# Branch A's queries as a third Strassen chunk, gates multiplied outside the streamed matmuls, and low weight halves made by accumulating DMAs

## The chip, the cores and the metric

One program runs on one core of a Trainium2 chip. The metric is the device time of an execution in microseconds, from its first to its last instruction with what lies around them; lower is better. A kernel's time is the median of three runs.

## The reference, cut to what matters

One layer of a decoder trunk: 512 tokens of width 2048, everything in fp32. One wide projection feeds three attention branches (A sparse, B latent, C over 256 memory tokens), each branch output is multiplied with SiLU of its own gate path z, projected to 2048, weighted with a sigmoid merge gate, summed, and projected out with a residual.

```python
h = rms_norm(x, norm_g[l])
proj = h @ w_in[l]                                   # 512x2048 @ 2048x13712
(aq, ak, av, az, iq, ik, iw, bcq, bckv, bkpe, bz, cq, cz, gates) = jnp.split(proj, IN_OFFSETS, axis=-1)
aq = rms_norm(aq.reshape(bsz, seq, A_HEADS, A_HEAD_DIM), a_q_norm_g[l])
o_a = dsa_attention(aq, ak, av, iq, ik, iw, positions, rel_bias).reshape(bsz, seq, A_WIDTH)
qb = (rms_norm(bcq, b_q_lat_norm_g[l]) @ w_b_uq[l]).reshape(bsz, seq, B_HEADS, B_QK_DIM)
kv = (rms_norm(bckv, b_kv_lat_norm_g[l]) @ w_b_ukv[l]).reshape(bsz, seq, B_HEADS, B_NOPE + B_V)
...
o_b = mla_attention(qb, kb, vb).reshape(bsz, seq, B_WIDTH)
mkv = rms_norm(mem, mem_norm_g[l]) @ w_mem_kv[l]
o_c = memory_attention(cq, ck, cv).reshape(bsz, seq, C_WIDTH)
u = jnp.stack([o_a * jax.nn.silu(az), o_b * jax.nn.silu(bz), o_c * jax.nn.silu(cz)], axis=2)
y_br = jnp.einsum('bsnw,nwd->bsnd', u, w_branch[l])
g = jax.nn.sigmoid(gates.reshape(bsz, seq, N_BRANCH, d))
merged = jnp.einsum('bsnd,bsnd->bsd', g, y_br)
x = x + merged @ w_out[l]
```

## The kernel before, in words

**Numbers in halves.** Every streamed product is made of three matmuls in a faster 32-bit format: each operand x is split into a high half (a copy into that format) and a low half (x minus the high half), and high·high, high·low and low·high are added up in PSUM. Activations are split once. Weights are split as they stream in: SP loads a tile of two 128-row blocks by 512 columns (`wraw`, 512 KB), ACT copies it to `whi`, DVE subtracts to get `wlo` (`split`).

**The stream.** `stream()` walks a list of chunks. A chunk is one block of 512 output columns; a job is one weight tile of it. A plain job is 24 matmuls of 128x512 (2 row blocks, 4 PSUM banks of ring `pg`, 3 products). A Strassen chunk takes two column blocks at once and forms 7 products where 8 would be needed, on sums of weight quarters that DVE makes from the raw tiles; its jobs are 12 matmuls. `LOOK` says how many jobs ahead of the matmuls the halves are prepared: 2 for a plain job, 3 for a Strassen job; `whi` and `wlo` have 3 buffers each, with one more (`extra`) for every fourth Strassen job.

**The order of chunks.** Memory keys and values; the first half of the indexer's queries; `bckv`; the Strassen chunks (cq0, cq1) and (bcq, akv) from `rows_chunk`; six Strassen chunks for the merge gates; the indexer's second half; uq and ukv (B's up-projections); **aq0 and aq1** (A's queries, plain, 16 row blocks each); the z chunks C0, C1, A0, A1, B0, B1; twelve branch chunks (four each for C, B, A, 8 row blocks each); two Strassen out chunks. The attention of C, B and the indexer runs between the matmuls of the stream up to the end of the z chunks, A's heads in the branch chunks of C and B.

**What sets the order.** `run` takes one step of the stream at a time and, after each, lets the attention threads go on as far as a planner's clock finds their data ready. The order of every engine and of every DMA queue is fixed by that when the program is built; each engine, and each queue, then works strictly in that order. SP carries the weight loads; the Pool queue carries spills to DRAM, reloads and attention loads.

**The end of a chunk.** `evac` empties the four banks of `pg`; the next chunk begins in the same four banks, in turn, right behind. In a z chunk each bank takes a tanh on ACT and a multiply-add on DVE, (tanh(z/2)+1)·z, which is twice SiLU. `silu_to_dram` (A's z before) stores that in DRAM as `sp_s`. `gated_chunk` (C's and B's z before) goes on: the attention output o comes back from DRAM (`zo`), `gated` multiplies, `halves` splits, and the two halves of u are stored as `sp_u`. `u_thread` later loads u for C (on SP) and B (on Pool); for A it loads s and o into `u_s` and `u_o`, multiplies and splits there.

**Between B and A.** When B's last head is done, A's preparation is issued on the Pool queue: positions (`pi`, `ki`), bias tables (`rb`), keys and values (`akv`), then the first A queries (`a_q`). The tile of `pi` takes memory that the B heads used, so its DMA waits for the last store of B's output (`sp_oB`).

**Names in the rows.** All instructions are recorded through one helper, so all have line 140; they are told apart by tiles. `hh`, `hl` are the halves of h, `hS` Strassen sums of it; `pg`, `pn` PSUM rings of the stream; `pa`, `pb`, `ra` those of attention; `mE`, `mO`, `mA` the halves for the out chunks; `wT` weight sums for these, made in DRAM and in part by accumulating DMAs on the Pool queue.

## Time and profile before

| | |
|---|---|
| time, median of three runs | 1877.44 us (1874.31, 1877.44, 1878.06) |
| profiled execution, own time | 1878.15 us |
| its span | 1876.3 us |
| PE busy | 1852.0 us (99%), 9341 matmuls |
| DVE, ACT, POOL busy | 1375.1 (73%), 860.7 (46%), 219.9 us (12%) |
| mean granted TensorE clock | 0.998 |
| DMA | 372.95 MB; the hardware queue of SP 37.0%, the software queue of Pool 25.1% of 16 engines' span |

PE is the engine that sets the time: what it does not spend in matmuls is 24.3 us of 1876.3. An engine's busy time elsewhere matters only where PE stands waiting for it. In rows of a timeline the bracket at the end tells how long the engine was idle before that instruction and what ended the wait; matmuls are pipelined, so that the distance between two starts, not the duration, is what one takes.

### The profile page before, as it was taken

How to read it: one execution, taken by the hardware profiler on the slowest of the kernel's cores; microseconds unless marked ns; L12 is line 12 of the kernel's file. 1: busy time of each engine (PE TensorE's matmuls, PEld its weight loads, DVE VectorE, ACT ScalarE, POOL GpSimd, SP SyncE). 2: the span in 40 equal slices, each digit the busy share in tenths (PEclk: the TensorE clock that was granted, in tenths of full speed). 3: DMA queues.
4: the chain of work that ended last, by engine and by line, in shares of the span. 5: the costliest groups of instructions: out<-in, count | busy, mean ns of one | idle time of the engine just before them, and what ended most of it. 6: DMA issues, size and time to landing. Idle time of an engine off the chain costs nothing. (4 is left out here: it accounts for less than half of the span.)

```text
span 1876.3 us, 25087 instructions
## 1 busy us (share of the span) xinstructions
PE 1852.0 (99%) x9341; PEld 1546.2 (82%) x9341; DVE 1375.1 (73%) x2156; ACT 860.7 (46%) x1429; POOL 219.9 (12%) x332
## 2 busy tenths in 40 slices
PE   8999999999999999999999999999999999999999
PEld 6789888888888888879888888878888888887787
DVE  5577877778777786765567789994788886667655
ACT  6543554454444444436846654433332324244442
POOL 1000010100001101021211111002012121210000
PEclk9999999999999999999999999999999999999999
DMA  7754558867667697575734435435565665946783
GB/s 263 248 183 143 163 188 317 205 210 213 188 194 290 225 254 202 173 240 164 262 111 142 129 113 180 149 109 166 171 239 191 200 215 175 316 158 211 259 270 123
DMA packets 155049, 372.95 MB, mean 199 GB/s; under 512 B 14560, under 2 KB 19568, under 8 KB 153648
## 3 DMA queue, kind: packets, MB, share of 16 engines
q1 hardware_dynamic: 111696, 220.36, 37.0%
q0 software_dynamic: 43200, 150.99, 25.1%
q8 instruction: 73, 1.20, 0.3%
q14 instruction: 48, 0.39, 0.1%
q10 hardware_dynamic: 32, 0.01, 0.0%
HBM read 308.63 MB, written 96.24 MB: 216 GB/s over the span
## 5 line engine op out<-in xcount | busy, mean ns | idle before, releaser
L140 DVE TENSOR_TENSOR wlo<-wraw,whi 128x1024 fp32r<-128x1024 f32 (+2 forms) x285 | 344.2, 1210 | 214.6 <-ACT whi L140 212.6
L140 ACT ACTIVATE whi<-wraw 128x1024 fp32r<-128x1024 f32 (+2 forms) x285 | 297.6, 1047 | 383.6 <-PE pg L140 160.2
L140 PE MATMUL pg<-whi,u 128*128 128x512 f32 x640 | 218.3, 400 | 0.0
L140 PE MATMUL pg<-hh,whi 128*128 128x512 f32 x512 | 207.0, 404 | 2.5 <-DVE stage L140 1.7
L140 PE MATMUL pg<-hh,wlo 128*128 128x512 f32 x512 | 200.7, 392 | 0.0
L140 PE MATMUL pg<-hl,whi 128*128 128x512 f32 x512 | 200.0, 391 | 0.0
L140 PE MATMUL pg<-whi,hh 128*128 128x512 f32 x384 | 151.8, 395 | 0.0
L140 PE MATMUL pg<-whi,hl 128*128 128x512 f32 x384 | 149.8, 390 | 0.0
L140 PE MATMUL pg<-wlo,hh 128*128 128x512 f32 x384 | 149.6, 390 | 0.0
L140 PEld LDWEIGHTS pg<-whi,u 128*128 128x128 f32 x640 | 120.3, 188 | 23.2 <-DVE yg L140 0.3
L140 ACT ACTIVATE whi<-sraw 128x1024 fp32r<-128x1024 f32 x79 | 83.2, 1058 | 98.5 <-DVE sraw L140 45.4
L140 DVE TENSOR_TENSOR wlo<-sraw,whi 128x1024 fp32r<-128x1024 f32 x79 | 96.4, 1224 | 42.5 <-ACT whi L140 42.1
L140 PE MATMUL pn<-whi,hS 128*128 128x512 f32 x384 | 126.0, 389 | 0.0
L140 PE MATMUL pg<-whi,hS 128*128 128x512 f32 x384 | 126.0, 389 | 0.0
L140 PE MATMUL pg<-wlo,u 128*128 128x512 f32 x320 | 125.1, 391 | 0.8 <-DVE wlo L140 0.8
L140 PE MATMUL pn<-whi,hl 128*128 128x512 f32 (+1 forms) x320 | 121.4, 379 | 0.0
L140 PE MATMUL pn<-wlo,hh 128*128 128x512 f32 (+1 forms) x320 | 121.4, 379 | 0.0
L140 PE MATMUL pn<-whi,hh 128*128 128x512 f32 (+1 forms) x320 | 121.4, 379 | 0.0
L140 PEld LDWEIGHTS pg<-hh,whi 128*128 128x128 f32 x512 | 96.8, 189 | 21.9 <-DVE stage L140 2.6
L140 PEld LDWEIGHTS pg<-hh,wlo 128*128 128x128 f32 x512 | 96.4, 188 | 21.1
L140 PEld LDWEIGHTS pg<-hl,whi 128*128 128x128 f32 x512 | 96.8, 189 | 17.3
L140 DVE TENSOR_TENSOR wlo<-T,whi 128x1024 fp32r<-128x1024 f32 x64 | 78.2, 1222 | 33.9 <-ACT whi L140 33.7
(450 smaller groups left out, 3956.9 us busy)
## 6 DMA issues: line engine op xcount, KB each, us to landing
wraw<-w_in SPq DMA_DIRECT2D x161, 512.0 KB, 3.9
sraw<-w_in SPq DMA_DIRECT2D x79, 512.0 KB, 4.5
wT<-w_out POOLq DMA_DIRECT2D x24, 1024.0 KB, 20.5
wraw<-w_branch SPq DMA_DIRECT2D x48, 512.0 KB, 4.4
wraw<-w_mem_kv SPq DMA_DIRECT2D x32, 512.0 KB, 5.3
yg<-sp_g POOLq DMA_DIRECT2D x24, 512.0 KB, 6.1
so<-wT SPq DMA_DIRECT2D x20, 512.0 KB, 5.7
wT<-wT POOLq DMA_DIRECT2D x8, 1024.0 KB, 13.8
```

Source lines behind the costliest of these rows:

```text
L140: return f(*a, **k)
```

## The change

Five things are done at once.

1. aq0 and aq1 leave the plain list and become a third `rows_chunk`, behind (bcq, akv) and ahead of the merge gates. `C0` gets the start condition that aq0 had.
2. `gated_chunk` is gone. All six z chunks (C, A, B as before) end in `silu_to_dram`. `u_thread` loads s and o, on SP, into the four `stage` buffers, and `gate` multiplies and splits them, for all three branches, shortly ahead of the branch chunk that reads u.
3. For the six z chunks (48 jobs) and the branch chunks of C and B (32 jobs), marked `dma`, the low halves come from `halves_by_dma`: ACT copies raw to `whi`, ACT writes −`whi` into `wlo`, and a DMA on the Pool queue that accumulates adds the raw weights, read from DRAM a second time, to `wlo`. `add_upto` issues it two jobs ahead of the job's matmuls. The DVE subtraction of these 80 jobs is gone.
4. `LOOK` is 3 for all jobs; `whi` and `wlo` have 4 buffers everywhere; `so` has 2 instead of 4; the flag `m sums` is gone.
5. The outputs of the attention heads are stored by ACT's DMA queue instead of Pool's, and the tile `o` is that of the probabilities.

The whole program has 9293 matmuls in place of 9341 (all of the 48 are 128x512 ones of the stream), 192 `wlo` subtractions on DVE in place of 269, and 80 more copies to `wlo` on ACT. On the Pool queue 80 accumulating DMAs of 512 KB come in, and 8 stores of `sp_s`; 16 stores of `sp_u`, 4 loads of u, 8 of `zo`, 8 of `u_s` and `u_o` and 40 stores of o go. On SP's queue 24 loads of s and o come in and 4 of u go; ACT's queue gets the 40 stores.

```diff
 class Kern:
-    LOOK = 2
+    LOOK = 3
...
+        def new_pair():
+            return [self.wp.tile([P, 2, 512], F32R, name=n, tag=n, bufs=4) for n in ("whi", "wlo")]
+
+        def halves_by_dma(jb, src):
+            h, l = new_pair()
+            nc.scalar.activation(h, src, AF.Copy)
+            nc.scalar.activation(l, h, AF.Copy, scale=-1.0)
+            jb["hl"] = (h, l)
+            (w,), row = jb["raws"][0]
+            st["adds"].append((st["nprep"], lambda: nc.gpsimd.dma_start(
+                l, w[row:row + 2 * P, :].rearrange("(k p) c -> p k c", p=P), accum_op=OP.add)))
+
+        def add_upto(n):
+            while st["adds"] and st["adds"][0][0] <= n:
+                st["adds"].pop(0)[1]()
+
         def halves(jb, src, w):
-            if jb.get("extra") and jb["ready"]:
-                h, l = [self.bp.tile([P, 2, 512], F32R, name=n, tag="yg", bufs=2) for n in ("whi", "wlo")]
-            else:
-                pool, bufs = (self.gp, 1) if jb.get("extra") else (self.wp, 3)
-                h = pool.tile([P, 2, 512], F32R, name="whi", tag="whi", bufs=bufs)
-                l = pool.tile([P, 2, 512], F32R, name="wlo", tag="wlo", bufs=bufs)
+            h, l = new_pair()
             self.split(h[:, :, :w], l[:, :, :w], src)
...
-            prep_upto(ji + 1 + min(self.LOOK + strassen, ji))
+            prep_upto(ji + 1 + min(self.LOOK, ji))
...
+            add_upto(ji + self.LOOK - 1)
...
-                pr = til([P, nblk * P], F32, "pr", 1 + tp)
+                pr = til([P, nblk * P], F32, "pr")
...
-            o = til([P, 256], F32, "o")
+            o = pr[:, :256]
             nc.scalar.activation(o, po.rearrange("p a b -> p (a b)"), AF.Copy)
             self.flags.add("B%d %d" % (tp, h))
-            nc.gpsimd.dma_start(self.sp["oB%d" % (h // 4)][:, h % 4, tp * 256:(tp + 1) * 256], o)
+            nc.scalar.dma_start(self.sp["oB%d" % (h // 4)][:, h % 4, tp * 256:(tp + 1) * 256], o)
...
         self.u = {}
-        yield "z half"
-        for n in (2, 1):
+        for n in (2, 1, 0):
             self.u[n] = []
+            last = None
+            if n == 2:
+                yield "z half"
             for k in range(4):
...
+                s, o = self.stage(), self.stage()
                 c, b = divmod(2 * k, 4)
...
+                nc.sync.dma_start(s, self.sp["s%d%d" % (n, c)][:, b:b + 2])
+                if k == 0:
+                    for x in (("C",), ("B part 0", "B part 1"), ("A",))[2 - n]:
+                        yield x
+                nc.sync.dma_start(o, self.sp["o%s%d" % ("ABC"[n], c)][:, b:b + 2])
...
+    def gate(self, n, k, s, o):
+
+        yield [s, o]
+        self.nc.vector.scalar_tensor_tensor(o, s, 0.5, o, op0=OP.mult, op1=OP.mult)
+        if n < 2:
+            yield "u%d out %d" % (n + 1, k)
+        u = self.u_tile(k)
+        yield [o]
+        self.split(u[:, 0], u[:, 1], o)
+        self.u[n].append(u)
+        self.flags.add("u%d%d" % (n, k))
...
+        self.rows_chunk(["aq0", "aq1"], [AQ, AQ + 512], [
+            [(j * P, j * P + P, lambda b, h=4 * c + j: one(self.a_ss[:, b], h)) for j in range(4)] for c in range(2)])
         for n in range(3):
             self.spill_tile("g%d" % n, NT, D)
...
-        for c in range(2):
-            sums = [(j * P, j * P + P, lambda b, h=4 * c + j: one(self.a_ss[:, b], h)) for j in range(4)]
-            self.chunk(win[:, AQ + c * 512:AQ + (c + 1) * 512], KT, 512, self.act_h, "tm", 4,
-                       self.to_dram("aq%d" % c, 4, 512, sums=sums))
...
+        for n in (2, 0, 1):
+            for c in range(2):
...
+                self.chunk(win[:, col:col + 512], KT, 512, act, "fm", 4, self.silu_to_dram("s%d%d" % (n, c)))
+                self.chunks[-1]["dma"] = True
...
         for i, n in enumerate((2, 1, 0)):
             for c in range(4):
                 self.branch_chunk(i, n, c)
+                self.chunks[-1]["dma"] = i < 2
```

The Pool queue between B and A, before. `pi`, `ki` and `rb` are A's small inputs, `akv` its keys and values, `zo` B's output on its way back for the gating, `a0_q` the first queries; the names carry buffer numbers.

```order
L140 DMA ki_11193<-positions 32x4x32
L140 DMA rb_11194<-rel_bias 32x8
L140 DMA rb_11194<-rel_bias 31x8
L140 DMA akv_11209<-sp_akv_133 128x2048
L140 DMA zo_11313<-sp_oB0_150 128x1024
L140 DMA zo_11314<-sp_oB0_150 128x1024
L1304 MEMSET tab_11338 128x96
L140 DMA a0_q_11494<-sp_aq0_146 128x256
L140 DMA a0_q_11496<-sp_aq0_146 128x256
```

The same place in the changed kernel; `wlo<-w_in` are the accumulating DMAs for z chunk B1, `wlo<-w_branch` that for the first branch chunk.

```order
L140 DMA ki_11538<-positions 32x4x32
L140 DMA rb_11539<-rel_bias 32x8
L140 DMA rb_11539<-rel_bias 31x8
L140 DMA akv_11554<-sp_akv_133 128x2048
L140 DMA wlo_11487<-w_in 128x2x512
L140 DMA wlo_11569<-w_in 128x2x512
L1275 MEMSET tab_11631 128x96
L140 DMA wlo_11600<-w_in 128x2x512
L140 DMA wlo_11692<-w_branch 128x2x512
L140 DMA a0_q_11776<-sp_aq0_134 128x256
```

The loads of `zo` are gone from there, and four accumulating DMAs stand behind `akv`, so behind the whole preparation of A; the first of them, `wlo_11487`, is used by the 69th matmul behind the last matmul of B's last head (the 68 between are stream matmuls on tiles that are complete by then).

ACT at the end of the first z chunk (C0), before: `zs<-pg` is the tanh of a bank, `zo<-zs` the high half of u, the rest belongs to B's heads.

```order
L140 ACTIVATE b1_o_9584<-pb1_9564 128x256
L140 ACTIVATE zs_9590<-pg_8956 128x512
L140 ACTIVATE b_qh_9595<-pb0_9602,g_bqn_635 128x512
L140 ACTIVATE zs_9590<-pg_8957 128x512
L140 ACTIVATE zs_9624<-pg_8958 128x512
L140 ACTIVATE zs_9624<-pg_8959 128x512
L140 ACTIVATE whi_9633<-wraw_9390 128x1024
L140 ACTIVATE zo_9280<-zs_9590 128x1024
L140 ACTIVATE zo_9281<-zs_9624 128x1024
L140 ACTIVATE whi_9676<-wraw_9480 128x1024
```

ACT at the same place in the changed kernel, where `stage<-pg` is the tanh.

```order
L140 ACTIVATE i_s1_8811<-i_q_8669 64x512
L140 ACTIVATE whi_8821<-wraw_8562 128x1024
L140 ACTIVATE wlo_8822<-whi_8821 128x1024
L140 ACTIVATE b_qs_8789<-pb0_8797 64x512
L140 ACTIVATE b_rh_8790<-pb0_8797 64x512 x2
L140 ACTIVATE b_kh_8787<-pb1_8834,g_bkn_735 128x512
L140 ACTIVATE b_vh_8783<-b_kv_8417 128x512
L140 ACTIVATE stage_8862<-pg_8156 128x512
L140 ACTIVATE stage_8862<-pg_8157 128x512
L140 ACTIVATE stage_8874<-pg_8158 128x512
L140 ACTIVATE stage_8874<-pg_8159 128x512
L140 ACTIVATE whi_8883<-wraw_8675 128x1024
```

The halves of u are gone, a second pass (`wlo<-whi`) stands behind each `whi`, and four tiles of the next B head (`b_qs` to `b_vh`) now stand directly ahead of the four tanh; on DVE the matching subtractions `b_kl` and `b_vl` stand directly ahead of the multiply-adds of the four banks.

DVE shortly before the out chunks, before: `m` is the merged sum turned into operands `mA`, `mE`, `mO`; `wlo` are halves of the out weights.

```order
L140 TENSOR_TENSOR wlo_15449<-wraw_15285,whi_15448 128x1024
L140 TENSOR_TENSOR wlo_15455<-so_15287,whi_15454 128x1024
L140 SCALAR_TENSOR_TENSOR mA211_15481<-pg_15466,mA210_15480 128x512
L140 TENSOR_TENSOR m_15410<-m_15410,m_15229 128x2x128
L140 TENSOR_TENSOR m_15229<-m_15229 128x2x128
L140 TENSOR_TENSOR m_15229<-m_15410,m_15229 128x2x128
L140 TENSOR_TENSOR m_15410<-m_15229,m_15410 128x2x128
L140 TENSOR_TENSOR mE_15492<-m_15229,mE_15491 128x512
L140 TENSOR_TENSOR mO_15496<-m_15410,mO_15495 128x512
L140 TENSOR_TENSOR wlo_15500<-so_15289,whi_15499 128x1024
```

The same place in the changed kernel.

```order
L140 TENSOR_TENSOR wlo_15539<-so_15344,whi_15538 128x1024
L140 SCALAR_TENSOR_TENSOR mA211_15565<-pg_15550,mA210_15564 128x512
L140 TENSOR_TENSOR m_15500<-m_15500,m_15321 128x2x128
L140 TENSOR_TENSOR m_15321<-m_15321 128x2x128
L140 TENSOR_TENSOR m_15321<-m_15500,m_15321 128x2x128
L140 TENSOR_TENSOR m_15500<-m_15321,m_15500 128x2x128
L140 TENSOR_TENSOR mE_15576<-m_15321,mE_15575 128x512
L140 TENSOR_TENSOR mO_15580<-m_15500,mO_15579 128x512
L140 TENSOR_TENSOR wlo_15584<-wraw_15381,whi_15583 128x1024
```

Of the two subtractions `wlo` that stood side by side ahead of the first group of m, one now stands earlier, in the branch chunk; the row `wlo<-so` or `wlo<-wraw` behind `mO` is the one that the first product on `mE` reads.

## Rows read from the trace of the kernel before

**Rows 1.** The page's first part: busy us (share) and instructions of PE and others

```profile
PE 1852.0 (99%) x9341; PEld 1546.2 (82%) x9341; DVE 1375.1 (73%) x2156; ACT 860.7 (46%) x1429; POOL 219.9 (12%) x332
```

**Rows 2.** Stretches: us, busy (count) of PE PEld DVE ACT POOL, PEclk, DMA, GB/s

```profile
300.00:400.00 100.00, 100.00 (x443) 82.81 (x442) 78.44 (x74) 49.94 (x71) 8.11 (x9) 1.00 0.82 242
```

**Rows 3.** What PE waited for: us in total, times, longest

```profile
PE pg L140 <- DVE wlo L140: 3.8, 5, 0.8
PE pb L140 <- DMA g_rows<-mem_norm_g: 3.7, 1, 3.7
PE pg L140 <- ACT whi L140: 2.9, 3, 1.9
PE pb L140 <- DMA px<-mem: 2.4, 1, 2.4
PE pa L140 <- DVE c_kl L140: 2.2, 1, 2.2
PE pg L140 <- DVE stage L140: 1.7, 1, 1.7
```

**Rows 4.** Timeline of PE: start us, us, instruction, idle before and its releaser

```profile
1178.60 0.50 PE L140 MATMUL pg<-hh,whi 128*128 128x512 f32 x1 [0.76 <-DVE zs L140]
1231.97 0.50 PE L140 MATMUL pg<-hh,whi 128*128 128x512 f32 x1 [1.69 <-DVE stage L140]
1731.59 0.50 PE L140 MATMUL pg<-whi,mE 128*128 128x512 f32 x1 [1.89 <-ACT whi L140]
```

**Rows 5.** Stretches behind two waits, columns as in rows 2

```profile
1231.00:1241.00 10.00, 9.03 (x44) 7.38 (x45) 8.99 (x18) 3.13 (x6) 1.11 (x2) 1.00 0.48 159
1731.00:1741.00 10.00, 7.79 (x23) 5.51 (x24) 8.83 (x13) 7.43 (x11) 1.42 (x2) 0.83 0.46 146
```

**Rows 6.** The page's fifth part: groups, busy and mean ns, idle before

```profile
L140 DVE TENSOR_TENSOR wlo<-wraw,whi 128x1024 fp32r<-128x1024 f32 (+2 forms) x285 | 344.2, 1210 | 214.6 <-ACT whi L140 212.6
L140 ACT ACTIVATE whi<-wraw 128x1024 fp32r<-128x1024 f32 (+2 forms) x285 | 297.6, 1047 | 383.6 <-PE pg L140 160.2
```

**Rows 7.** Tile zs: duration ns min/median/max, first and last start, form

```profile
L140 ACT ACTIVATE zs<-pg x16: 587/600/609, 1119.8 to 1388.3; 128x512 f32<-128x512 f32 x16
L140 DVE SCALAR_TENSOR_TENSOR zs<-zs,pg x16: 676/680/689, 1120.4 to 1389.1; 128x512 f32<-128x512 f32 x16
```

**Rows 8.** Timelines of PE, ACT and POOL where B's last head ends

```profile
1292.06 0.27 PE L140 MATMUL pb<-b_ph,b_vl 128*128 128x128 f32 x1
...
1292.37 0.38 ACT L140 ACTIVATE b_o<-pb 128x256 f32<-128x256 f32 x1 [2.29 <-PE pb L140]
...
1293.05 0.54 POOL L140 DMA_DIRECT2D sp_oB<-b_o  x1 [2.08 <-ACT b_o L140]
1296.78 0.54 POOL L140 DMA_DIRECT2D pi<-positions  x1 [3.19 <-DMA sp_oB<-b_o]
...
1304.76 0.56 POOL L140 DMA_DIRECT2D akv<-sp_akv  x1
```

**Rows 9.** Tile wT from 345 to 385 us: four accumulating DMAs of 1 MB

```profile
L140 POOL DMA_DIRECT2D wT<-w_out x4: 1264/1602/2372, 348.7 to 359.5; - x4
...
DMA to landing us min/median/max: 10.5/21.2/25.4
```

**Rows 10.** DMA issues of the page: count, KB each, median us to landing

```profile
sp_s<-stage POOLq DMA_DIRECT2D x4, 512.0 KB, 4.0
```

**Rows 11.** Stretches with their DMA share, columns as in rows 2

```profile
345.00:372.00 27.00, 27.00 (x120) 22.36 (x120) 21.85 (x20) 12.90 (x21) 5.90 (x6) 1.00 0.99 241
1321.00:1571.00 250.00, 250.00 (x1767) 205.35 (x1767) 205.04 (x471) 84.82 (x154) 44.21 (x67) 1.00 0.60 202
```

**Rows 12.** Timelines of ACT, DVE and PE where A's last head ends

```profile
1593.75 0.39 ACT L140 ACTIVATE a_o<-ra 128x256 f32<-128x256 f32 x1 [3.59 <-PE ra L140]
...
1605.84 1.23 DVE L140 TENSOR_TENSOR u<-u_s,u 128x1024 fp32r<-128x1024 f32 x1 [1.12 <-ACT u L140]
...
1617.33 0.39 PE L140 MATMUL pn<-whi,u 128*128 128x512 f32 x1
```

More of the change, by code (lines that the diff above doesn't have):

```diff
@@ L333, in stream @@
             jobs += self.jobs_of(ci, c)
-        for ji, jb in enumerate(x for x in jobs if "kp" in x["c"]):
-            jb["extra"] = ji % 4 == 3
-            jb["ready"] = isinstance(jb["c"]["w"], dict)
+        for jb in jobs:
+            jb["ready"] = "kp" in jb["c"] and isinstance(jb["c"]["w"], dict)
         loads, tags = [], {}
@@ L342, in stream @@
                 if jb.get("ready"):
[L343 removed]
+                    tag = "wraw" if nstr % 5 < 3 else "so"
                     nstr += 1
@@ L400, in prep @@
                 i, = jb["lids"]
-                halves(jb, raw[i][:, :, :w], w)
+                if c.get("dma"):
+                    halves_by_dma(jb, raw[i])
+                else:
+                    halves(jb, raw[i][:, :, :w], w)
                 done(i)
@@ L440, in prep_upto @@
                     return
-                if jb.get("extra") and jb["ready"] and "m sums" not in self.flags:
-                    return
                 load_some(99)
@@ L1677, in u_thread @@
-        yield "A"
-        def load(k):
-            s, o = [self.bp.tile([P, 2, 512], F32, name="u_" + x, tag="so", bufs=4) for x in "so"]
-            c, b = divmod(2 * k, 4)
-            nc.gpsimd.dma_start(s, self.sp["s0%d" % c][:, b:b + 2])
-            nc.gpsimd.dma_start(o, self.sp["oA%d" % c][:, b:b + 2])
-            return s, o
-        ahead = [load(0), load(1)]
-        self.u[0] = []
-        for k in range(4):
-            s, o = ahead.pop(0)
-            yield [s, o]
-            nc.vector.scalar_tensor_tensor(s, s, 0.5, o, op0=OP.mult, op1=OP.mult)
-            yield "u1 out %d" % k
-            u = self.u_tile(k)
-            self.u[0].append(u)
-            yield [s]
-            self.split(u[:, 0], u[:, 1], s)
-            if k < 2:
-                ahead.append(load(k + 2))
-            self.flags.add("u0%d" % k)
+                nc.sync.dma_start(s, self.sp["s%d%d" % (n, c)][:, b:b + 2])
@@ new lines, in u_thread @@
+                if k == 0:
+                    for x in (("C",), ("B part 0", "B part 1"), ("A",))[2 - n]:
+                        yield x
+                nc.sync.dma_start(o, self.sp["o%s%d" % ("ABC"[n], c)][:, b:b + 2])
+                if last:
+                    yield from self.gate(n, k - 1, *last)
+                last = s, o
+                if n == 2:
+                    yield from self.gate(n, k, *last)
+                    last = None
+            if last:
+                yield from self.gate(n, 3, *last)
@@ L1747, in add @@
                     nc.vector.tensor_tensor(m, box["m"][b // 2][:, b % 2], g, op=OP.add)
-                    if b == 3 and c == 3:
-                        self.flags.add("m sums")
                 self.defer(add, b == 3, 1)
@@ L2033, in build @@
                 self.spill_tile("o%s%d" % (key, c), 4, 512)
-        for c in range(2):
-            self.gated_chunk(2, c)
-        for c in range(2):
-            col = AZ + c * 512
-            self.chunk(win[:, col:col + 512], KT, 512, self.act_h, "fm", 4, self.silu_to_dram("s0%d" % c))
-        for c in range(2):
-            self.gated_chunk(1, c)
+        for n in (2, 0, 1):
+            for c in range(2):
+                col = (AZ, BZ, CZ)[n] + c * 512
+                act = self.act_h
+                if n == 1 and c == 1:
+                    act = lambda k: (k == 8 and self.flags.add("z half"), self.act_h(k))[1]
+                self.chunk(win[:, col:col + 512], KT, 512, act, "fm", 4, self.silu_to_dram("s%d%d" % (n, c)))
+                self.chunks[-1]["dma"] = True
+                if n == 2 and c == 0:
+                    self.chunks[-1]["start"] = "kpe"
+                    pre(lambda: (lpool.close(), self.flags.add("latents done")))
         self.chunks[-1]["post"] = close_h
```

57 lines of the change are left out of this document (5 added, 52 removed).

## The prediction

> **What bounds the kernel now.** I read the page's busy shares first: PE works 1852.0 of 1876.3 us [rows 1], so the kernel is a list of matmuls with 24.3 us of holes. Second the stretches: where PE never waits, 443 matmuls of the stream take 100 us [rows 2], 0.2257 us each; that is the price of one matmul taken away or added. Third, what PE waited for [rows 3]: small items, most of them at the beginning (gains and memory tokens from DRAM, 6.1 us, which the change leaves alone), the rest where a chunk ends or the out chunks begin. Two such waits have a place that the change touches: 0.76 and 1.69 us at the ends of two z chunks and 1.89 us at the start of the out chunks [rows 4]. Fourth the clock behind a wait: after the 1.69 us wait the granted clock stayed 1.00, after the 1.89 us wait the ten microseconds hold a mean of 0.83 [rows 5], so 0.17 × 10 = 1.7 us are lost once more, at the lower of the two levels. A wait of some two microseconds thus costs nearly twice its length here. So an edit counts by two things only: stream matmuls, and waits of PE.
>
> **DVE's subtractions** are not such a thing. 80 of them go, 80 × 1.21 = 97 us of DVE; 80 further ACT passes come, 80 × 1.05 = 84 us [rows 6]. DVE is at 73% and ACT at 46% of the span [rows 1], and the only waits of PE for `wlo` are 3.8 us in five pieces [rows 3]. Neither is worth more than what it does to a PE wait; what matters is the third link that the 80 jobs get, a DMA that must land.
>
> **1. Queries by Strassen.** Two plain chunks of 16 row blocks are 2 × 16 × 4 × 3 = 384 matmuls; as one Strassen chunk 7/8 of that, 336. The 48 that go are the difference of the program's matmul counts, and all lie in the saturated stream: 48 × 0.2257 = **−10.8 us**. DVE pays for the weight sums, in a stage that already runs at 443 matmuls in 100 us with the same work for the other Strassen chunks [rows 2], so they are hidden. The attention of C, B and the indexer, which ran beside aq0 and aq1 too, now runs beside fewer stream matmuls; its own matmuls are the same.
>
> **2. The Pool queue between B and A.** Before, nothing that the stream needs soon stood behind A's preparation. Now the add for `wlo_11487` does, and 68 stream matmuls, 68 × 0.2257 = 15.3 us, are all that PE has between B's last matmul and it. The chain, from the trace: B's last matmul ends at 1292.33, ACT copies until 1292.75, the store is issued at 1293.05 and `pi`, which waits for it to land, starts at 1296.78 [rows 8]: 4.5 us. From ACT's queue the store saves the hop, so I take 3.6 to 4.5. From `pi` to the end of the issue of `akv` are 1305.32 − 1296.78 = 8.5 us, all of it issue work in Pool's order, unchanged. Then the add has to land. The trace has only accumulating DMAs of 1 MB: the first landed 10.5 us after its issue at 348.7; four of them were down by 359.5 + 25.4 = 384.9 at the latest, so each further one took (384.9 − 359.2) / 3 = 8.6 us, and half a megabyte alone should take about 10.5 − 4.3 = 6.2 us (estimate) [rows 9]. Together 18.3 to 19.2, a wait of 3.0 to 3.9 us; with `akv`'s megabyte ahead of it on the same queue up to some 6.5. If an add lands as fast as a plain half megabyte from the same queue, 4.0 us [rows 10], the wait is 0.8 to 1.7. I take 4.7, nearer to the accumulating rows, and 1.7 for the clock, since it is longer than 1.89: **+6.4 us**, between 0 and 10. The next add is behind by 4.3 us and has 24 matmuls, 5.4 us, more to go, so it does not wait again.
>
> The Trainium skill, "DMA: Bandwidth & Descriptors", section "Anatomy of one DMA — SWDGE (gpsimd) path", fits one DMA of this queue as 2.0 us plus its bytes over 436,000 per us and makes no difference for accumulating ones, which would be 3.2 us for 512 KB. By that the chain is 15.3 to 16.2 us, there is next to no wait and the sum comes out about 6 us lower; the trace's accumulating rows, 8.6 us per megabyte, speak against it.
>
> **3. The ends of the z chunks.** A chunk's banks are reused in turn: behind the last matmul on the first bank PE has 9 matmuls, 2.0 us, until it writes that bank anew. In that time ACT's tanh (0.60) and DVE's multiply-add (0.68) must be through [rows 7], which leaves 0.7 us. Before, the six ends cost 0.76 + 1.69 = 2.45 us. In the change the worst is the end of C0: ACT has a `whi` and a `wlo` (2.1 us) and some seven tiles of 0.6 us of B's head ahead of the first tanh, from the transposes for `b_qh` on, about 8.5 us to the end of that tanh and 0.9 to the end of the multiply-add, against 7.5 us of PE work from there: about 2 to 2.5 us of wait, just long enough for the clock's 1.7. A second end has a similar knot of about 1.6, the others together 1. So 2.5 + 1.7 + 1.6 + 1.0 − 2.45 = **+4.3 us**; the bounds are 0 (the two waits of before come back in other places) and +8. What speaks for less: the gating and the halves of u, four passes of about 1.2 us on DVE and two of about 1.05 on ACT per chunk by the rates of [rows 6], have left these places.
>
> **4. The start of the out chunks.** DVE's chain to the first `mE` product has one subtraction less at its head, 1.21 us [rows 6], so the 1.89 us wait [rows 4] becomes 0.7, and 1.69 was short enough for the clock to stay. I take 1.2 + 0.7, **−1.9 us**, between 0 and −3.6 (all of the wait and all of the clock).
>
> **5. The rest.** In the memory chunks PE waits for `whi` and `wlo` in pieces under 0.8 us [rows 3]; one job more of lead takes off **−0.8** (0 to −1.8). Elsewhere adds are issued two jobs ahead, 10.9 us without attention in between, against 6.2 to land; the tightest leads, some ten where a spill or a load stands ahead in the Pool queue, are 9.4 us. I put **+1** for one or two that miss. Where A ends: before, from `a_o` at 1593.75 to the end of the first split 1607.07 are 13.3 us, and PE reads the first of A's u at 1617.33 [rows 12], 10 us of cover to spare; now some 12 us of PE work stand between the last A matmul and that read, but the first tile of u needs only outputs that are stored long before, so **0** (0 to +3). The store on ACT's queue and the single probability buffer for B cost an issue on ACT each, 40 in all, beside idle time: 0.
>
> **Sum.** −10.8 + 6.4 + 4.3 − 1.9 − 0.8 + 1.0 = −1.8 us against the profiled span of 1876.3, so 1874.5. A run's own time is 1.85 above its span (1878.15) and that run was 0.7 above the median of 1877.44: a median of about **1875.5 us**. A measurement of this kernel can tell about 0.2%, 3.75 us, from no change; this forecast lies within.
>
> **Rivals.** *A, the adds are cheap and the knots hidden.* If an accumulating half megabyte lands like a plain one (4.0 us, the size also of the rule quoted above) term 2 falls to about +0.8, and the sum is 1870; if the ends of the z chunks are no worse than before as well, 1865. For it: DVE, on which the knots of before ended (`zs`, `stage`), loses 97 us of work. Against it: the rows of the 1 MB adds, and B's operands straight ahead of the tanh in the order.
>
> *B, slower: the DMA engines saturate in the branch chunks.* There the share was 0.60 over 250 us [rows 11], and 32 adds come in. At 8.6 us per megabyte each costs 4.3 us at most (weight loads ran beside them), 138 us or 0.55 of the stretch; the sum is 1.15, and the engines are full from 0.40 × 250 / 32 = 3.1 us for one add on. The stretch with the four adds stood at 0.99 and PE lost nothing, but for 27 us only [rows 11]. The point from which it decides is an add that lands more than 9.4 us after its issue: then the ten tight places wait, some 1 to 2 us each, and the longer ones take the clock along. That is +10 to +23, 1886 to 1898.
>
> *C, A's end is late.* If the last outputs of A, now loaded on SP behind weight loads, hold the first splits, 3 to 5 us come on top: 1879 to 1881.
>
> *D, it does not do what it says.* The 48 matmuls are gone from the program, so this holds for the adds only: DVE's time buys nothing anywhere. That is the forecast with term 4 at 0, 1877.
>
> **How the numbers follow.** Forecast with D 45% (own range 1870 to 1881), A 28% (1864 to 1870), B 20% (1883 to 1898), C 7%. Faster by over 0.2% (below 1873.7): A and 0.08 of the forecast, 0.36. Slower (above 1881.2): B, 0.03 of C and 0.01, 0.24. Within: 0.40. The range from 1865 to 1887 leaves out about a tenth at the bottom, where everything is hidden, and a tenth at the top, the heavier half of B.
>
> **What would show it.** Term 1: a saturated stretch of about 54 us for the third Strassen chunk early on, and 48 matmuls fewer. Term 2: a wait of PE for a DMA `wlo<-w_in`, 3 to 6 us long, some 15 us behind B's last matmul, with the granted clock at its lower level behind it. Term 3: waits for `stage` on DVE at the beginning of the second z chunk. Term 4: the wait at the first `mE` product below 1.7 us and the clock at 1.00 behind it. If the forecast is wrong, the landing of `wlo` is the first thing to look at: near 4 us says A, above 9 us B. A DMA share near 1.00 in the branch chunks together with many short waits for `wlo` would say B too; waits for `u` or `stage` ahead of the last four branch chunks, C.

## The result and the profile after

The changed kernel takes 1891.2 us (median; 1889.88 to 1894.51) against 1876.89 us for the kernel before (four runs of each): ratio 1.0081, 95% interval 1.0063 to 1.0098. It is 14.3 us slower where about 2 us of gain were forecast (1875.5 against the 1877.44 known then), and lies above the range.

The page's first part of the changed kernel, as [rows 1]:

```profile
PE 1850.9 (98%) x9293; PEld 1539.8 (81%) x9293; DVE 1323.3 (70%) x2110; ACT 955.3 (51%) x1521; POOL 278.4 (15%) x344
```

The profiled run has a span of 1889.6 us, 13.3 more than before. PE stands idle for 38.7 us where it was 24.3. Its busy time falls by 1.1 us only, although 48 matmuls are gone: the mean clock is 0.995 in place of 0.998, which is 9.4 − 3.8 = 5.7 us. So −10.8 (matmuls) + 14.4 (waits) + 5.7 (clock, from rounded means) leaves about 4 us more of PE's busy time; no row tells where they lie.

What PE waited for, us in total, times, longest, as [rows 3]:

```profile
PE pg L140 <- DVE stage L140: 8.7, 7, 2.9
PE pg L140 <- DMA wlo<-w_in: 7.6, 1, 7.6
PE pb L140 <- DMA g_rows<-mem_norm_g: 4.6, 1, 4.6
...
PE pa L140 <- DMA ikw<-sp_bckv: 2.3, 1, 2.3
PE pg L140 <- DVE yg L140: 1.9, 3, 1.0
```

Where the larger ones stand, PE's timeline, as [rows 4]:

```profile
1078.14 0.79 PE L140 MATMUL pg<-hh,whi 128*128 128x512 f32 x1 [2.86 <-DVE stage L140]
1155.72 0.50 PE L140 MATMUL pg<-hh,whi 128*128 128x512 f32 x1 [2.04 <-DVE stage L140]
1214.69 0.50 PE L140 MATMUL pg<-hh,whi 128*128 128x512 f32 x1 [1.08 <-DVE stage L140]
1368.28 0.79 PE L140 MATMUL pg<-hh,wlo 128*128 128x512 f32 x1 [7.57 <-DMA wlo<-w_in]
1391.11 0.51 PE L140 MATMUL pg<-whi,u 128*128 128x512 f32 x1 [1.89 <-DVE stage L140]
1745.36 0.51 PE L140 MATMUL pg<-whi,mE 128*128 128x512 f32 x1 [1.06 <-ACT whi L140]
```

The wait for the indexer's weights `ikw`, three stretches of 4 us that begin at such waits' ends (that of `ikw` first), and the stretch of the branch chunks of C and B (columns as in [rows 2]):

```profile
1051.43 0.63 PE L140 MATMUL pa<-ident,ikw 128*64 128x128 f32 x4 [2.34 <-DMA ikw<-sp_bckv]
...
1051.40:1055.40 4.00, 3.97 (x23) 3.44 (x24) 2.03 (x4) 3.22 (x6) 0.29 (x1) 1.00 0.78 147
1155.70:1159.70 4.00, 3.98 (x12) 3.27 (x13) 2.50 (x4) 1.74 (x4) 3.74 (x5) 0.61 0.87 260
1391.10:1395.10 4.00, 3.99 (x27) 3.19 (x27) 4.00 (x9) 2.20 (x3) 3.02 (x3) 0.63 0.51 105
1392.00:1620.00 228.00, 226.07 (x1652) 185.54 (x1652) 171.32 (x446) 111.19 (x183) 70.59 (x79) 0.99 0.94 258
```

Behind the waits of 2.04 and 1.89 us the clock was down, which lost 4 × 0.39 and 4 × 0.37 or 1.5 to 1.6 us, as in [rows 5]. The length of the wait alone does not decide it: behind the 2.34 us for `ikw` the clock stayed at 1.00. The DMA share in the last stretch is 0.94 where a similar stretch had 0.60 [rows 11].

By place, with 1.7 us for each fall of the clock:

| place | before: wait + clock | after: wait + clock | change |
|---|---|---|---|
| 48 stream matmuls | | | −10.8 |
| beginning, first 110 us | 9.9 | 8.3 | −1.6 |
| start of the attention | 2.2 + 1.7 | 0.8 | −3.1 |
| ends of the z chunks (and of the chunk ahead of them) | 2.5 | 9.1 + 5.1 | +11.7 |
| indexer weights `ikw` | 0.2 | 2.3 | +2.1 |
| between B and A | 0 | 7.6 + 1.7 | +9.3 |
| merge gates `yg` in the branch chunks | 0 | 1.9 | +1.9 |
| start of the out chunks | 3.4 + 1.7 | 2.6 + 1.7 | −0.8 |

That adds up to +8.7; the remaining 4.6 of the 13.3 are, but for 0.6 of clock, the 4 us from above that have no place. Two places carry the loss.

The chain between B and A, from the timelines of PE, ACT's queue and POOL, as [rows 8]:

```profile
1344.94 0.27 PE L140 MATMUL pb<-b_ph,b_vl 128*128 128x128 f32 x1
...
1345.66 0.33 ACTq L140 DMA_DIRECT2D sp_oB<-b_pr  x1
...
1350.45 0.61 POOL L140 DMA_DIRECT2D pi<-positions  x1 [12.58 <-ACT whi L140]
...
1357.75 0.56 POOL L140 DMA_DIRECT2D akv<-sp_akv  x1
1358.29 2.53 POOL L140 DMA_DIRECT2D wlo<-w_in  x2
```

5.2 us from B's last matmul to `pi` (its row names ACT's `whi`, not the store, as what came last), 7.9 to the end of the issue of `akv`, then 10.0 until PE goes on at 1368.28: 23.1 us against 15.3 of cover.

### The profile page after: what moved, and what is told of

Read it like the earlier page. It is cut to its first block, busy times and chain, and to the rows that moved or that the text cites. A ratio compares the mean times of both kernels' runs of the same rounds, so it can differ in the third digit from the quotient of the medians.

```text
span 1889.6 us, 25158 instructions
## 1 busy us (share of the span) xinstructions
PE 1850.9 (98%) x9293; PEld 1539.8 (81%) x9293; DVE 1323.3 (70%) x2110; ACT 955.3 (51%) x1521; POOL 278.4 (15%) x344
## 4 chain that ended last, share of the span: by engine, by line
PE 85%; DMA 5%; DVE 4%; ACT 4%; issue 2%; POOL 0%; ACTq 0%; DVEq 0%; POOLq 0%
PE pg L140 51%; PE pn L140 25%; PE pb L140 3%; PE pa L140 3%; DMA wraw<-w_mem_kv 2%; PE ra L140 2%; ACT whi L140 2%; DVE wlo L140 1%; PE rb L140 1%; ACT junk L140 1%; DMA stage<-sp_oB 1%; DMA b_q<-sp_uq 1%; DMA wlo<-w_in 1%; DVE stage L140 0%; ACT stage L140 0%
## 5 line engine op out<-in xcount | busy, mean ns | idle before, releaser
L140 DVE TENSOR_TENSOR wlo<-wraw,whi 128x1024 fp32r<-128x1024 f32 (+2 forms) x208 | 250.2, 1205 | 150.9 <-ACT whi L140 149.6
L140 PE MATMUL pg<-whi,hS 128*128 128x512 f32 x448 | 147.0, 389 | 0.0
L140 DVE TENSOR_TENSOR wlo<-sraw,whi 128x1024 fp32r<-128x1024 f32 x90 | 109.9, 1224 | 50.5 <-ACT whi L140 49.8
L140 PE MATMUL pn<-whi,hl 128*128 128x512 f32 (+1 forms) x352 | 133.9, 380 | 0.0
L140 PE MATMUL pn<-wlo,hh 128*128 128x512 f32 (+1 forms) x352 | 133.9, 380 | 0.0
L140 PE MATMUL pn<-whi,hh 128*128 128x512 f32 (+1 forms) x352 | 133.9, 380 | 0.0
L140 PE MATMUL pg<-wlo,hh 128*128 128x512 f32 x288 | 112.2, 389 | 0.0
L140 PE MATMUL pg<-whi,hl 128*128 128x512 f32 x288 | 112.1, 389 | 0.0
L140 PE MATMUL pg<-whi,hh 128*128 128x512 f32 x288 | 112.0, 389 | 0.0
L140 ACT ACTIVATE whi<-T 128x1024 fp32r<-128x1024 f32 x72 | 76.2, 1059 | 69.3 <-DVE T L140 25.2
```

Source lines behind the costliest of these rows:

```text
L140: return f(*a, **k)
```

## The experiments

The changed kernel does several things at once, so the first four runs separate its main parts: Strassen for A's queries, the adds, and the rest (gates apart, four buffers, a lead of three jobs). Ratios are against the kernel before in the same batch, 1874.0 to 1875.2 us.

**e1: Strassen queries alone, on the kernel before.**

```diff
+        self.rows_chunk(["aq0", "aq1"], [AQ, AQ + 512], ...)
-        for c in range(2):
-            self.chunk(win[:, AQ + c * 512:AQ + (c + 1) * 512], KT, 512, self.act_h, "tm", 4, ...)
```

> The kernel before with aq0 and aq1 as a third Strassen chunk and nothing else of the change. Theory ADDS (the 24 us that the change gives away come with the low halves made by DMA: their queue and their extra ACT pass): 48 matmuls less and no new wait, 1877 - 10.8 = 1866 us. Theory CROWDING (taking matmuls out from beside the attention leaves ACT and DVE less time per matmul, so that chunk ends wait): 3 to 8 us come back as waits at the ends of the z chunks, 1869 to 1874 us.

Measured 1924.3 us, ratio 1.026 (1.0244 to 1.0276): 49 us slower. CROWDING had the direction, but neither the size nor the place. PE's largest waits:

```profile
PE pn L140 <- ACT u L140: 11.0, 1, 11.0
PE rb L140 <- DVE bm L140: 8.4, 4, 5.3
PE ra L140 <- DVE bm L140: 7.2, 4, 2.5
```

All at A's end. How full DVE is (the third busy column) from the end of z chunk C0 (in e1, of C1) to about B's last head in the kernel before, in e1, and in the changed kernel, one row each:

```profile
1122.00:1292.00 170.00, 167.51 (x839) 138.60 (x837) 153.55 (x325) 71.55 (x121) 15.98 (x27) 1.00 0.43 138
...
1150.00:1350.00 200.00, 196.48 (x976) 162.15 (x975) 179.62 (x390) 85.08 (x149) 17.10 (x29) 0.99 0.41 134
...
1078.00:1345.00 267.00, 263.07 (x1342) 219.62 (x1343) 194.93 (x472) 161.95 (x274) 59.84 (x61) 0.99 0.78 187
```

DVE is busy for 90% of that stretch in the first two and for 73% in the third. Before, it was full here already; two chunks of 192 matmuls, 87 us of PE work beside which the attention could run, are taken away from there, and the attention's work does not become less. It ends later than the stream that should cover it, and PE stands: this stretch of stream matmuls was its cover.

**e2: no adds, all low halves by DVE.**

```diff
-                self.chunks[-1]["dma"] = True
-                self.chunks[-1]["dma"] = i < 2
```

> The changed kernel with every low half subtracted on DVE, no accumulating DMA. ADDS: the 7.6 us wait for wlo<-w_in and its slow clock (9.3 us) go, and with the extra ACT pass gone the waits at the z chunk ends fall to the 2.5 us of before: 1891 - 9.3 - 8 = 1874 us or less. CROWDING: only the 9.3 us go, the z chunk ends stay at 9 us of wait or grow since DVE has 97 us more to do: 1882 to 1886 us.

Measured 1911.8 us, ratio 1.02 (1.0183 to 1.0217): 20 us worse than the changed kernel. The late add is gone, and in its place:

```profile
PE pg L140 <- DVE stage L140: 13.5, 7, 9.6
PE ra L140 <- DVE bm L140: 5.3, 2, 2.6
PE ra L140 <- DVE a_q L140: 4.4, 2, 4.0
```

ADDS falls; CROWDING has the direction, but 1882 to 1886 us was too little. The adds are what makes Strassen queries bearable.

**e3: the changed kernel with plain queries. e4: the same without adds too.** Both put the two plain chunks back where they stood; e4 also has the edit of e2.

> The changed kernel with aq0 and aq1 as two plain chunks where they stood before. ADDS: 48 matmuls come back and the waits stay, 1891 + 10.8 = 1902 us. CROWDING: attention has its 88 us of stream matmuls beside it again, the z chunk ends lose most of their waits, 1892 to 1895 us.

> The changed kernel without accumulating DMAs and with plain queries: what is left is the gating apart from the streamed matmuls, four uniform buffers for the halves and a lead of three jobs. ADDS: about the kernel before, 1874 to 1880 us. CROWDING: the same or a little less, 1872 to 1878 us, since the attention has its cover again; the two theories differ in e2 minus e4, which is -10.8 us by ADDS and between 0 and -5 us by CROWDING.

e3 gives 1902.4 us (1.0148; 1.0133 to 1.0163), e4 1880.8 us (1.0028; 1.0016 to 1.0039). The four together:

| | low halves by DVE | by adding DMAs |
|---|---|---|
| plain queries | 1880.8 (e4) | 1902.4 (e3) |
| Strassen queries | 1911.8 (e2) | 1891.2 (changed) |

Each part alone costs, 31 us for Strassen and 22 for the adds; together they cost 10. With the adds, Strassen brings its full 11 us. Neither theory had this: e2 minus e4 is +31, where they allowed −11 to 0, although e3 alone came out at ADDS's 1902. Each of these kernels was also planned anew, so every figure contains what the planner made of its edit. e18 below changes one number of the planner and nothing else, and that moves 14 us: the 31 and the 49 of e1 stand well clear of this, the smaller figures less so or not at all. PE's largest waits in e3:

```profile
PE pg L140 <- DMA wlo<-w_in: 7.2, 1, 7.2
PE pg L140 <- DVE stage L140: 5.5, 9, 1.0
PE pg L140 <- DMA wlo<-w_branch: 4.7, 3, 2.5
PE pg L140 <- DVE yg L140: 4.3, 4, 2.3
```

Of the 5.5 us for `stage`, 5.0 lie at the ends of the z chunks, and the clock does not fall there. The changed kernel has 9.1 + 5.1 at these places and the chunk end ahead of them: with its cover the attention disturbs them less. What e3 gains there it loses in the branch chunks, to `wlo` (4.7) and `yg` (4.3), so the full 11 us are a balance.

The rest of the change, e4, is some 5 us slower than the kernel before (1875.2); its profiled run, 1877.8, is among the quickest of its ten (1876.9 to 1883.7) and has no more waiting than the kernel before, so where these 5 us lie stays open.

**e5 to e8: the two places, taken away.** e5 loads A's small inputs and `akv` on SP's queue. e6 issues each add three jobs ahead. e7 lets no attention thread go on during the last job of a z chunk. e8 is e5 and e7.

```diff
-        nc.gpsimd.dma_start(pi, ...)
+        nc.sync.dma_start(pi, ...)
```

```diff
-            add_upto(ji + self.LOOK - 1)
+            add_upto(ji + self.LOOK)
```

```diff
-                    yield
+                    yield "hold" if c.get("hold") and jb["last"] else None
...
+            elif r == "hold":
+                if self.later:
+                    self.later.pop(0)()
```

> The changed kernel with A's small inputs and akv (pi, ki, rb, akv) loaded on SP's queue in place of Pool's. Theory KNOT (the 7.6 us wait for wlo<-w_in is Pool's order behind pi): the wait and its slow clock go, 1891 - 9 = 1882 us. Rival: the waiting pi now holds SP's weight loads for the 5 us until B's output has landed, and the next halves are late instead: 1888 to 1892 us.

> The changed kernel with each accumulating DMA issued three jobs ahead of its matmuls in place of two. KNOT: the add that was late now stands before pi, the next one stays behind it and has 5.4 us more cover, so 7.6 us become about 2 and the clock stays up: 1883 to 1885 us. If the adds were late because the DMA engines are full, nothing is gained, 1890 to 1893 us.

> The changed kernel with the attention threads held during the last job (24 matmuls) of each z chunk, so that no operand of theirs stands on ACT and DVE directly ahead of the evacuation. Theory ORDER (the z chunk ends wait because B's and the indexer's operands stand ahead of tanh and multiply-add): of 8.2 us of waits for stage and 5.2 us of slow clock at them about 2 us remain: 1880 to 1883 us. Theory CROWDING: ACT and DVE have too little time in this stretch, the work held back makes others wait as long: 1888 to 1893 us.

> e5 and e7 together. KNOT and ORDER both true: 1891 - 9 - 10 = 1872 us, below the kernel before; one of them true: 1880 to 1883 us; neither: about 1890 us.

Measured: e5 1899.3 (1.0135; 1.0117 to 1.0153), e6 1925.9 (1.0267; 1.0248 to 1.0287), e7 1893.8 (1.0102; 1.0087 to 1.0117), e8 1896.7 us (1.0116; 1.0101 to 1.0131). None is faster than the changed kernel; e7's interval overlaps that of the changed kernel, 1.0063 to 1.0098. e7 is the clearest. The waits for `stage` on DVE have gone from 8.7 to 0.5 us, so they do come from operands that stand ahead of the evacuation; but now

```profile
PE pg L140 <- DMA wlo<-w_branch: 7.6, 1, 7.6
...
PE ra L140 <- DVE bm L140: 2.6, 1, 2.6
PE ra L140 <- DVE a_ql L140: 2.4, 1, 2.4
PE pn L140 <- ACT u L140: 2.0, 1, 2.0
```

The work that was held back is missing at A's end, where the changed kernel had no wait. ORDER is right on the cause and wrong on the gain. In e5, e6 and e8 the planner, whose books saw other queue times, also set another order behind the edit; they don't tell what the edit itself does. In e5 and e8 the late add is gone, and PE waits instead at A's first transposes (4.3 and 6.1 us) and for ACT's halves of u (7.4 and 17.7 us); in e6 the late add still costs 4.3 us, and u 15.2.

**e9 to e11: earlier adds in an unchanged order.** e9 issues the adds one job earlier and books them in the planner where they stood, so that every engine but Pool keeps the order of the changed kernel. e10 and e11 hold the attention as in e7, at all z chunks or at C's two.

```diff
+            st["adds"].append((st["nprep"], lambda: nc._nc.gpsimd.dma_start(l, src, accum_op=OP.add)))
+            st["books"].append((st["nprep"], lambda: self.plan.call(
+                lambda *a, **k: None, "q_pool", "dma_start", (l, src), dict(accum_op=OP.add))))
...
+            while st["adds"] and st["adds"][0][0] <= n + 1:
```

> As e6, each accumulating DMA one job earlier, but with the planner's books as in the changed kernel, so that every engine's order but Pool's is that of the changed kernel. KNOT: the 7.6 us wait for wlo<-w_in shrinks to 0 to 3 us and the clock behind it stays up, all other waits stay as they are: 1882 to 1885 us. If e6 was slow because of earlier adds as such and not because of the other order, its waits for u return: 1915 to 1925 us.

> e9 with the attention held in the last job of every z chunk (as e7). ORDER: the waits for stage go and nothing takes their place, 1871 to 1875 us. CROWDING: the held work turns up at the end of A's attention as in e7 (8.4 us of waits there and slow clock): 1884 to 1890 us.

> e9 with the attention held only in the last job of z chunks C0 and C1, whose ends cost 2.9 and 2.0 us and 3.4 us of slow clock. ORDER: 8 us less than e9, 1874 to 1877 us. CROWDING: a third of the held work of e10, so a smaller wait at A's end, 1878 to 1885 us.

Measured: e9 1904.6 (1.0162; 1.0147 to 1.0178), e10 1909.9 (1.0197; 1.018 to 1.0214), e11 1907.7 us (1.0179; 1.0163 to 1.0194). In e9 no add is late, and it is 13 us slower than the changed kernel; neither branch of its expectation holds:

```profile
PE pg L140 <- DVE yg L140: 7.4, 4, 4.0
PE rb L140 <- DVE akv L140: 6.7, 1, 6.7
PE pa L140 <- DMA ikw<-sp_bckv: 4.4, 1, 4.4
```

`yg` and `ikw` are loads of Pool's queue, for which PE already waited in the changed kernel (1.9 and 2.3 us). No other order has changed, so the adds that now stand ahead of them make them later. The wait for `akv` is another matter: e12 has it without any add.

e10 and e11 miss both of their branches too. The hold makes the wait for `akv` 9.9 and 8.5 us; e10 has e7's waits at A's end again, and in e11 PE waits at two later z chunk ends instead, 2.85 and 3.05 us.

**e12: the adds left out.** The low halves are then just minus the high halves; every other engine keeps its order.

```diff
-            st["adds"].append((st["nprep"], lambda: nc.gpsimd.dma_start(l, ..., accum_op=OP.add)))
+            st["adds"].append((st["nprep"], lambda: self.plan.call(
+                lambda *a, **k: None, "q_pool", "dma_start", (l, src), dict(accum_op=OP.add))))
```

> The changed kernel with the 80 accumulating DMAs left out (the low halves are then minus the high half; the order on every engine but Pool's queue is that of the changed kernel). Theory QUEUE (the adds are late themselves and make the loads behind them in Pool's queue late): the waits for wlo<-w_in (7.6 us and the slow clock), for ikw (2.3) and for yg (1.9) go, the z chunk ends stay: 1891 - 14 = 1877 us. If the DMA engines' load as a whole slows SP's loads too, more goes, 1870 us. If the adds cost only their own one wait: 1882 us.

Measured 1884.3 us (1.0048; 1.0031 to 1.0065): the 80 transfers cost 6 to 7 us as a whole, less than the 14 of QUEUE. The waits for `ikw` and the late add are gone, and of the 1.9 us for `yg` 1.0 is left. But:

```profile
PE pg L140 <- DVE stage L140: 8.7, 7, 2.9
PE rb L140 <- DVE akv L140: 6.1, 1, 6.1
```

The z chunk ends wait exactly as in the changed kernel, so the transfers have no part in them. And between B and A PE now waits 6.1 us for `akv`. PE's timeline of e12, from B's last matmul to A's first transposes, and the row of the kernel before that answers to the second (its B ends at 1292.06 [rows 8]):

```profile
1342.79 0.27 PE L140 MATMUL pb<-b_ph,b_vl 128*128 128x128 f32 x1
...
1369.66 1.09 PE L140 MATMUL rb<-ident,akv 128*128 128x128 f32 x4 [6.10 <-DVE akv L140]
```

```profile
1326.95 0.60 PE L140 MATMUL rb<-ident,akv 128*128 128x128 f32 x4
```

Before, 153 stream matmuls, 34.5 us, stood between the two; in the changed order there are 90, 20.3 us, and the chain takes 26.6. So the late add was only the first of two things for which PE would have stood at this place.

**e13: a plain copy for the add.** A plain DMA of the same 512 KB writes the raw weight to `wlo`; ACT's second pass and the accumulation are left out, so the low half is the raw weight.

```diff
-            nc.scalar.activation(l, h, AF.Copy, scale=-1.0)
...
+                nc._nc.gpsimd.dma_start(l, src)
```

> The changed kernel with a plain DMA of the same 512 KB to wlo in place of ACT's second pass and the accumulating DMA (the low half is then the raw weight), same order elsewhere. If accumulating is what makes the transfer slow (8.3 us against 4 to 6 for a plain one), the B-to-A wait of 7.6 us becomes 3 to 5 us; if ACT's second pass is what makes the z chunk ends late, their 8.2 us of waits fall to 3 or less: 1872 to 1876 us with both, 1884 to 1887 us with the first alone, 1891 us with neither.

Measured 1884.3 us (1.0047; 1.0029 to 1.0064). The issues of `wlo` (count, KB, median us to landing) of the changed kernel, then of e13, with e13's waits:

```profile
wlo<-w_in POOLq DMA_DIRECT2D x48, 512.0 KB, 8.2
...
wlo<-w_branch POOLq DMA_DIRECT2D x32, 512.0 KB, 9.1
```

```profile
wlo<-w_in POOLq DMA_DIRECT2D x48, 512.0 KB, 6.4
wlo<-w_branch POOLq DMA_DIRECT2D x32, 512.0 KB, 7.2
```

```profile
PE pg L140 <- DVE stage L140: 7.1, 7, 2.0
PE pg L140 <- DMA wlo<-w_in: 6.4, 1, 6.4
```

Accumulating costs some 1.8 us of landing, and a plain transfer would have been late as well: 6.4 us of wait. ACT's second pass is 1.6 us of the 8.7 at the chunk ends. The waits of neither branch came; that 1884.3 lies in the range for the first alone is chance.

**e14 and e15: the adds in one stage only**, in the z chunks or in the branch chunks (one of the two lines of e2 taken out).

> The changed kernel with the adds in the z chunks only, DVE subtracting in the branch chunks of C and B (39 us more of DVE there). CROWDING: A's attention waits for DVE at its end as in e2 (bm, a_q: some 13 us with the slow clock): 1898 to 1906 us. QUEUE: what the branch adds cost the yg loads comes back, 1886 to 1889 us.

> The changed kernel with the adds in the branch chunks of C and B only, DVE subtracting in the z chunks (58 us more of DVE there). CROWDING: B's heads and the indexer end later, A starts later and the first branch chunk waits for u as in e2 (9.6 us): 1898 to 1906 us. QUEUE: the late add between B and A and the late ikw go, 1880 to 1884 us.

Measured: e14 1910.7 (1.0189; 1.0174 to 1.0205), e15 1895.9 us (1.011; 1.0095 to 1.0126). e14 goes beyond the figure of CROWDING, with waits for `bm` and u at A's end. e15 is a little below its figure for CROWDING and far above that for QUEUE; its largest item is a single wait at the first branch chunk:

```profile
PE pg L140 <- DVE stage L140: 19.0, 7, 15.1
```

Both kernels were planned anew; with that caveat, both stages need the relief, the branch chunks more.

**e16 and e17: the chain between B and A shortened.** The 12 loads of `ki` and `rb` are issued before the attention begins, every other order unchanged (e16); with the hold of e7 (e17).

```diff
+            self.a_small()
...
-            nc.gpsimd.dma_start(ki[s * 32:(s + 1) * 32], ...)
-            nc.gpsimd.dma_start(rb[s * 32:(s + 1) * 32, 0], rel)
```

> The changed kernel with the 12 loads of ki and rb (and rb's memset) issued before the attention begins, into memory of their own; every other engine's order is that of the changed kernel. Theory COVER (from B's last matmul to A's first transposes there are 90 stream matmuls, 20.3 us, where there were 153, 34.5 us, and the chain pi to akv takes 27 us): the chain loses 7 us of issue work, the wait of 7.6 us at wlo<-w_in falls to 1 to 2 with the clock staying up and no wait for akv takes its place: 1881 to 1884 us. If the time saved comes back behind it as in e9: 1888 to 1892 us.

> e16 with the attention held in the last job of every z chunk (as e7). If A now begins 7 us sooner, the held work has room and A's end no longer waits 8 us: the z chunk ends' 8 us and their slow clock come off, 1869 to 1875 us, at or below the kernel before. CROWDING: A's end still waits as in e7, 1881 to 1886 us.

Measured: e16 1897.8 (1.0122; 1.0107 to 1.0138), e17 1896.0 us (1.0121; 1.0104 to 1.0138). The chain does what was expected and the time does not. PE's timeline of e16, and the row of DVE behind its second large wait:

```profile
900.30 0.45 PE L140 MATMUL pb<-ident,lraw 128*128 128x128 f32 x1 [2.88 <-issue]
...
1365.29 0.50 PE L140 MATMUL pg<-hh,wlo 128*128 128x512 f32 x1 [1.44 <-DMA wlo<-w_in]
...
1387.98 0.80 PE L140 MATMUL pg<-whi,u 128*128 128x512 f32 x1 [5.00 <-DVE stage L140]
...
1386.10 1.23 DVE L140 SCALAR_TENSOR_TENSOR stage<-stage 128x1024 f32<-128x1024 f32 x1 [6.61 <-DMA stage<-sp_oC]
```

7.57 us became 1.44. But the end of the last z chunk, 20 us later, now waits 5.00 us in place of 1.89: in DVE's order the gating of C's u stands ahead of that chunk's evacuation, and DVE itself waits 6.61 us for the reload of C's output. The early loads cost 2.88 us where they were put, which was a fault of this experiment. The profiled run, 1892.8 us, is the quickest of e16's four, 5 us below their median, so the trace does not show the whole loss. In e17 the ends of the z chunks no longer wait, and A's end does, as in e7 (`bm`, `a_ql`, u and `a_qh`, 8.5 us), besides 4.5 us for the first `wlo<-w_branch`.

**e18: one number of the planner.** From the merge gates on, attention threads are held when ACT or DVE lies 1.5 us behind, in place of 3.

> The changed kernel with one number of the planner changed from the merge gates on: attention threads are held while ACT's or DVE's planned work lies more than 1.5 us behind PE, in place of 3 us. The same work in another order. ORDER (the changed kernel was left in an order that could be better): the z chunk ends lose half of their waits and nothing of that size comes back, 1880 to 1885 us. CROWDING (work held back turns up as waits elsewhere, as in e7): 1889 us or more.

Measured 1904.9 us (1.0155; 1.0139 to 1.0172). The waits for `stage` fall to 4.7 us, the late add stays (8.3), and waits for u of 4.4 and 6.5 us appear in the first branch chunk and at A's end: as in e7, only more so.

## Why the prediction was wrong, point by point

**What bounds the kernel.** The reading was right that stream matmuls and waits of PE count, and that a wait of about two microseconds costs nearly twice its length where the clock falls behind it. The forecast took that from the wait's length, which does not decide it (2.34 us for `ikw`). Wrong was what I took from the reading, that DVE's subtractions "are not such a thing". Waits of the trace before tell what is late, not what is nearly late: DVE was 90% busy over the z chunks, and that row was not among those I rested on. Nor did DVE gain the 97 us: its busy time fell by 52. It still does 392 subtractions to `wlo` where it did 460 (192 and 269 are those of one form), and the third Strassen chunk brings it work, 36 us in e1.

**The step that failed** stands in **term 1**. Its −10.8 is the matmuls' true worth, but the sentence behind it, that the attention "now runs beside fewer stream matmuls; its own matmuls are the same", put the cover that goes with them at nothing. e1 prices it at 49 + 11 = 60 us when DVE keeps its subtractions, with the plan made for that kernel. In the changed kernel it shows in the size of term 3: the ends of the z chunks cost 5.0 us with the cover (e3, though in a plan of its own) and 9.1 + 5.1 without. The relief by the adds, 20 us beside Strassen queries (e2), I had priced at nothing as well. Two errors of opposite sign largely cancel, and that the forecast is no further off than 16 us is luck in that respect.

**Term 2** (+6.4, 0 to 10) became +9.3. The place, the engine and the order were right; the way to `pi` took 5.2 us in place of 3.6 to 4.5, and the add landed 9.95 us after its issue, not 6.2: my division of the 1 MB rows took the transfer to be alone. What the term missed is the second chain at the same place: in the changed order A's first transposes have 63 stream matmuls less ahead of them, so that without the add PE waits 6.10 us for `akv` in place of 7.57 (e12).

An estimate by the fit on the page "DMA: Bandwidth & Descriptors" of the Trainium skill, section "Anatomy of one DMA — SWDGE (gpsimd) path", puts this transfer at 3.2 us. The runs disagree: 8.2 and 9.1 us median for accumulating ones and 6.4 and 7.2 for plain ones of 512 KB beside this traffic. Rival A calls 4.0 us the size of that fit too, which it is not.

**Term 3** (+4.3, 0 to 8) became +11.7, above its bound; its 7.4 us too little are the largest part of what the sum missed. The first two ends came as worked out (2.86 and 2.04 for 2.5 and 1.6). "The others together 1" were 0.84 (the chunk ahead of C0), 1.08, 0.37 and 1.89, and the clock fell three times, not once. That operands ahead of the evacuation are the cause is shown by e7, where all but the 0.84 go; e12 clears the transfers, and e13 leaves ACT's second pass 1.6 us. That holding the operands back wins nothing is shown by e7 too.

**Term 4** (−1.9) became −0.8: the wait fell to 1.06 us, but 0.76 us more followed 1.3 us later, and the clock fell all the same. Those 0.76 us had stood behind the 1.89 us of before too, so that the 1.89 were not shown to bring the clock down by themselves. **Term 5:** the beginning gained 1.6 for 0.8; one add of 80 was late, at the place of term 2; A's end cost nothing. Not foreseen: `ikw` and `yg` behind the adds in Pool's queue (+4.0; e9 shows the cause, and without adds, in e12, 1.0 us for `yg` is left) and the start of the attention (−3.1).

**Rivals.** B names the right size for the wrong reason: the DMA share did rise to 0.94 over the branch chunks of C and B, yet there all adds landed in time. A is refuted by e12, which has no adds at all and is still 9 us slower than the kernel before. C did not come: PE waits for nothing at A's end. D, that DVE's time buys nothing, is refuted by e2.

**What stays open.** Whether a new order could make the changed program faster than the kernel before is not settled: ten attempts to take waits away (e5 to e11, e16 to e18) each moved them, and none of these runs is faster than the changed kernel. e7, e9, e16 and e17 show the way it goes: the wait removed is really gone, and the next chain, planned for the time at which the first one used to end, takes its place. No version beat the kernel before.

## What to carry to other kernels

A stretch of matmuls is not only work but also the cover of everything that is planned beside it: before taking matmuls out, add up what the other engines do in that stretch, from the row of the stretch and not from the span's share (DVE 90% there, 73% overall). When a step is moved between engines, list every place where a chain between two phases runs through the queue that it joins, and measure each such chain against the matmuls that are left to cover it, the second-longest too. In a kernel whose orders are fixed beforehand, test a suspected wait with all other orders held; otherwise the new plan is measured, not the edit.

## What the hardware showed that was not expected

An accumulating DMA of 512 KB landed 5.7 to 14.6 us after its issue (80 of them in the changed kernel, median 8.3), a plain one in its place 3.7 to 11.3 (e13, median 6.9). Its row on Pool lasted 1.2 us (median) and the plain one's 0.7, but where another issue stood behind it Pool began that after 0.7 us in both.

Two short waits of PE, 1.06 and 0.76 us with 0.5 us of work between them, were followed by the lower clock, while a single one of 1.69 us [rows 5] and one of 2.34 us were not. The same wait can go either way: at the end of z chunk C1, in the same order on PE, the clock fell to a mean of 0.61 over 4 us behind 2.04 us in the changed kernel, and stayed at 1.00 behind 2.03 us in e12:

```profile
1155.00:1159.00 4.00, 3.90 (x21) 3.37 (x22) 2.55 (x5) 1.83 (x4) 2.09 (x3) 1.00 0.78 274
```
